# Half-product operands built one step at a time, more pairs by seven half products, and two weight sums made by adding transfers

## The chip, the cores and the metric

The kernel runs on one core of a Trainium2 chip. The metric is the device time of one execution in microseconds (us). A core has a matrix engine (TensorE, PE in the rows; PEld is its weight load), a vector engine (VectorE, DVE), a scalar engine (ScalarE, ACT), a general engine (GpSimd, POOL) and SyncE (SP), which here only starts transfers.

## What is computed

Two decoder layers over 512 positions of width 1024, in float32. Layer 0 mixes with retention and sparse attention, layer 1 with a gated linear recurrence; both end with a SwiGLU feed-forward part, which is all that the change touches:

```python
def swiglu(h, w1, w3, w2):          # D_MODEL 1024, D_FF 2816
    return (jax.nn.silu(h @ w1) * (h @ w3)) @ w2
...
    h = rmsnorm(x, norm_ffn_g[layer])
    x = x + swiglu(h, ffn_w1[layer], ffn_w3[layer], ffn_w2[layer])
```

## The kernel before

**Precision.** Each float32 operand is split into a rounded high part and a low remainder, and a product is three matmuls: high weights by high data (L129), high by low (L130), low by high (L131). `load_split` (L105) loads 512 KB of weights into one of two `raw` buffers (L109, SyncE), casts 128x512 halves to `whi` on ACT (L116) and subtracts to get `wlo` on DVE (L118).

**The feed-forward part.** `ffn` goes over 22 pairs f of 128 columns of w1 and w3, in two halves of 11; each half ends with `residual_out`, 8 blocks of 33 matmuls that multiply by w2. A pair comes in two forms. The *normal* form projects twice (`p_a`, `p_b`): 2 x 8 x 3 = 48 matmuls of 512 columns, with four casts and four subtractions of weights. Then DVE multiplies by the norm factor R (L357), ACT applies silu (L358), DVE makes g (L360), POOL multiplies g by R (L361), and g is split into `gh` and `gl` (L154, L155).

The *seven* form (`seven_products`) treats the two projections as a product of 2x2 block matrices and makes it from seven half products: 7 x 4 x 3 = 84 matmuls of 256 columns, with seven casts and seven subtractions of weights. Four of the seven weight operands are sums, `s1` to `s4`, of the halves a1, a2 (of the pair's `raw_a`) and b1, b2 (of `raw_b`), made on DVE: s1 = b1+b2 (L304), s2 = s1+a1 (L305), s3 = a1+b1 (L314), s4 = s2+a2 (L320). They lie in slab 4 for every other such pair, and in cells 22 to 25 for the rest. The products' results are put together on DVE in 256-column pieces (L313, L319, L325, L329 to L332), then silu (L333), g (L334), and g by R on POOL (L335). `SEVEN` lists the pairs of this form, 11 of 22 in each layer: 2, 4, 6, 8, 10, 11, 13, 15, 17, 19, 21.

On the data side the seven form needs sums of halves of the normalised input, `xu` and `xw`. `seven_operands` makes them once in each layer, for four k: for each k two ACT scalings (L257), four DVE operations of 256 columns (L260 to L263) and two splits (a cast on ACT, a subtraction on DVE, each). It is called ahead of pair 2, for all four k.

**Order.** A scheduler sets the order of each engine's instructions when the kernel is built, from the order of the code and from the buffers; each engine then works through its list strictly in order, and waits where an operand is not there. Transfers started from one engine are started in its order too.

Of the kernel before, what the change touches and what calls it, by code (L numbers as in the profile page):

```python
# [12 lines left out]
FR = mybir.dt.float32r  # L13
BF = mybir.dt.bfloat16
U8 = mybir.dt.uint8
AF = mybir.ActivationFunctionType
ALU = mybir.AluOpType
# [14 lines left out]
def trunk(ctx, tc, t_in, out):  # L32
    nc = tc.nc
# [12 lines left out]
    def slab(i, name, dt=F32):  # L46
        return big.tile([128, 4, 512], dt, name=name, tag=f"B{i}")

    def cell(i, name, dt=F32):
        return big.tile([128, 512], dt, name=name, tag=f"c{i}")  # L50

    def temp(name, dt=F32):
        return tmp.tile([128, 512], dt, name=name, tag="t")
# [16 lines left out]
    xT = [xall[:, k, :] for k in range(KT)]  # L70

    hh = [wp.tile([128, S], FR, name=f"hh{k}", tag=f"hh{k}", bufs=1) for k in range(KT)]
    hl = [wp.tile([128, S], FR, name=f"hl{k}", tag=f"hl{k}", bufs=1) for k in range(KT)]
    gains = main.tile([128, 5, KT], F32, name="gains")
# [78 lines left out]
    def split(dst_h, dst_l, src, eng=None):  # L153
        nc.scalar.copy(dst_h, src)  # L154
        (eng or nc.vector).tensor_tensor(out=dst_l, in0=src, in1=dst_h.bitcast(F32), op=ALU.subtract)  # L155
# [89 lines left out]

    SEVEN = [2, 4, 6, 8, 10, 11, 13, 15, 17, 19, 21]


    def seven_operands(layer, which):
        lo, hi = slice(0, 256), slice(256, 512)
        xs = {1: [], 2: [], 3: [], 4: [], 5: [], 6: [], 7: []}
        for k in range(4):
            x1, x2 = temp(f"x1_{layer}_{k}"), temp(f"x2_{layer}_{k}")
            for x, j in ((x1, k), (x2, k + 4)):
                nc.scalar.activation(out=x, in_=xT[j], func=AF.Copy, scale=gains[:, which, j:j + 1])  # L257
            u, w = temp(f"xu_{layer}_{k}"), temp(f"xw_{layer}_{k}")
            tt = nc.vector.tensor_tensor
            tt(out=u[:, lo], in0=x1[:, lo], in1=x1[:, hi], op=ALU.subtract)  # L260
            tt(out=u[:, hi], in0=x2[:, hi], in1=u[:, lo], op=ALU.add)
            tt(out=w[:, lo], in0=x2[:, lo], in1=u[:, hi], op=ALU.subtract)
            tt(out=w[:, hi], in0=x1[:, hi], in1=x2[:, hi], op=ALU.subtract)  # L263
            U, W = ([cell(6 + 4 * k + 2 * j + i, f"x{n}{layer}_{k}_{i}", FR) for i in range(2)]
                    for j, n in enumerate("uw"))
            split(*U, u)
            split(*W, w)
            for i, part, cs in ((1, (hh[k], hl[k]), lo), (2, (hh[k + 4], hl[k + 4]), lo),
                                (3, (hh[k + 4], hl[k + 4]), hi), (5, U, lo), (6, U, hi), (4, W, lo), (7, W, hi)):
                xs[i].append((part[0][:, cs], part[1][:, cs]))  # L270
        return xs

    def seven_products(layer, f, xs, norm, n):
        w13 = t_in["w13"]
        lo, hi = slice(0, 256), slice(256, 512)
        tt = nc.vector.tensor_tensor
        name = f"{layer}_{f}"
        ra, rb = (wp.tile([128, 1024], F32, name=f"raw_{x}{name}", tag="raw", bufs=2) for x in "ab")
        nc.sync.dma_start(out=ra, in_=w13[layer, 2 * f])
        nc.sync.dma_start(out=rb, in_=w13[layer, 2 * f + 1])  # L280
        a1, a2, b1, b2 = ra[:, 0:512], ra[:, 512:1024], rb[:, 0:512], rb[:, 512:1024]
        if n % 2:
            s1, s2, s3, s4 = (cell(22 + j, f"s{j}_{name}") for j in range(4))
        else:
            q = slab(4, f"s_{name}")
            s1, s2, s3, s4 = (q[:, j, :] for j in range(4))
        ws = {}

        def parts(i, src):
            ws[i] = load_split(None, 512, f"s{i}_{name}", [src])  # L290

        def product(i, o, first):
            ((wh_, wl_),) = ws[i]
            for j, (xh, xl) in enumerate(xs[i]):
                wh, wl = wh_[:, j * 128:(j + 1) * 128], wl_[:, j * 128:(j + 1) * 128]
                mm(o, wh, xh, start=first and j == 0, stop=False, skip_group_check=True)  # L296
                mm(o, wh, xl, start=False, stop=False, skip_group_check=True)  # L297
                mm(o, wl, xh, start=False, stop=j == 3, skip_group_check=True)  # L298

        t1, t2 = cell(26, f"t1_{name}"), cell(27, f"t2_{name}")  # L300
        p1, v, v7 = t1[:, lo], t1[:, hi], t2[:, lo]
        ta, g = temp(f"ta{name}"), temp(f"g{name}")
        parts(1, a1)
        tt(out=s1, in0=b1, in1=b2, op=ALU.add)  # L304
        tt(out=s2, in0=s1, in1=a1, op=ALU.add)  # L305
        o1 = bank("mm", f"p_w{name}")[:, lo]
        product(1, o1, True)
        nc.scalar.copy(p1, o1)
        parts(6, s2)
        o2 = bank("sc", f"p_x{name}")[:, lo]  # L310
        product(6, o2, True)
        parts(2, a2)
        tt(out=v, in0=o2, in1=p1, op=ALU.subtract)  # L313
        tt(out=s3, in0=a1, in1=b1, op=ALU.add)  # L314
        product(2, o1, False)
        parts(7, s3)
        product(7, o2, False)
        parts(5, s1)
        tt(out=v7, in0=o2, in1=p1, op=ALU.subtract)  # L319
        tt(out=s4, in0=s2, in1=a2, op=ALU.add)  # L320
        o3 = bank("sc", f"p_z{name}")[:, lo]
        product(5, o3, True)
        parts(4, b2)
        product(4, o2, False)
        tt(out=g[:, hi], in0=v7, in1=o3, op=ALU.subtract)  # L325
        parts(3, s4)
        product(3, o3, False)
        R = norm.R
        tt(out=ta[:, lo], in0=o1, in1=R[:, lo], op=ALU.mult)  # L329
        tt(out=g[:, lo], in0=o2, in1=p1, op=ALU.subtract)  # L330
        tt(out=ta[:, hi], in0=o3, in1=v, op=ALU.subtract)
        tt(out=ta[:, hi], in0=ta[:, hi], in1=R[:, hi], op=ALU.mult)  # L332
        nc.scalar.activation(out=ta, in_=ta, func=AF.Silu)  # L333
        tt(out=g, in0=g, in1=ta, op=ALU.mult)  # L334
        nc.gpsimd.tensor_tensor(out=g, in0=g, in1=R, op=ALU.mult)  # L335
        return g

    def ffn(layer, norm, norm_next, tail=None):
        w13, w2 = t_in["w13"], t_in["w2"]
        half = NF // 2  # L340
        for f0, f1 in ((0, half), (half, NF)):
            bh = [slab(i, f"gh{layer}_{f0}_{i}", FR) for i in range(2)]
            bl = [slab(2 + i, f"gl{layer}_{f0}_{i}", FR) for i in range(2)]
            gs = [(bh[j // 4][:, j % 4, :], bl[j // 4][:, j % 4, :]) for j in range(8)]
            gs += [(cell(2 * j, f"gh{layer}_{f0}_{j}", FR), cell(2 * j + 1, f"gl{layer}_{f0}_{j}", FR))
                   for j in range(half - 8)]
            for f in range(f0, f1):
                if f == 2:
                    xs = seven_operands(layer, norm.which)
                if f in SEVEN:  # L350
                    g = seven_products(layer, f, xs, norm, SEVEN.index(f))
                else:
                    a = project(w13[layer, 2 * f], f"a{layer}_{f}")
                    R = norm.R if norm.R is not None else norm.factor()
                    b = project(w13[layer, 2 * f + 1], f"b{layer}_{f}", tag="sc")
                    ta = temp(f"ta{layer}_{f}")
                    nc.vector.tensor_tensor(out=ta, in0=a, in1=R, op=ALU.mult)  # L357
                    nc.scalar.activation(out=ta, in_=ta, func=AF.Silu)  # L358
                    g = temp(f"g{layer}_{f}")
                    nc.vector.tensor_tensor(out=g, in0=b, in1=ta, op=ALU.mult)  # L360
                    nc.gpsimd.tensor_tensor(out=g, in0=g, in1=R, op=ALU.mult)  # L361
                split(*gs[f - f0], g)
            end = f1 == NF
            residual_out(w2[layer], f0, f1, gs, norm_next if end else None, f"y{layer}_{f0}_", tail if end else None)
# [53 lines left out]
    for s in range(2):  # L418
        kf = temp(f"kc{s}")
        nc.vector.tensor_tensor(out=kf, in0=first[s], in1=R0, op=ALU.mult)  # L420
        for g in range(2):
            for j2 in range(2):
                nc.sync.dma_start(out=kc2[2 * s + g][j2 * 64:j2 * 64 + 64, 0:S - j2],
                                  in_=kf[g * 64:g * 64 + 64, j2:S])
# [6 lines left out]
    for br in range(2):  # L431
        kf = temp(f"kf{br}")
        nc.vector.tensor_tensor(out=kf, in0=first[2 + br], in1=R0, op=ALU.mult)
        for part, dst in zip(parts(f"kf{br}", kf), (KA, KB)):
            for g in range(2):
                for h in range(2):
                    nc.sync.dma_start(out=dst[h * 64:h * 64 + 64, 2 * br + g, :].bitcast(F32),
                                      in_=part[g * 64:g * 64 + 64].bitcast(F32))
    VVr = VV.rearrange("p (b g) (c h d) -> p b g c h d", b=2, h=2, d=64)
    for br in range(2):  # L440
# [4 lines left out]
        for c in range(4):  # L445
# [4 lines left out]
                                op=ALU.subtract)  # L450
# [7 lines left out]
    for s in range(2):  # L458
        ph = bank("sc", f"h1_{s}")
        for half in range(2):  # L460
            x = cell(12 + 2 * s + half, f"xkv{s}{half}")[:, 0:496].rearrange("p (j g i) -> p j g i", j=8, g=2)
            for g in range(2):
# [3 lines left out]
                    out=x[:, :, g, :], in0=src,  # L466
                    in1=cpos[:, s, 8 * half:8 * half + 8].unsqueeze(2).to_broadcast([128, 8, 31]), op=ALU.add)
# [620 lines left out]
```

## Time and profile before

| | before |
|---|---|
| median of three runs (two of them 1339.71 and 1340.9) | 1340.9 us |
| the profiled execution | 1340.04 us |
| its span, first to last instruction | 1338.3 us |
| PE busy | 1312.1 us, 98% |
| DVE busy | 886.2 us, 66% |
| ACT busy | 581.6 us, 43% |
| POOL busy | 353.6 us, 26% |
| mean granted clock of TensorE | 0.990 of full speed |

Busy shares are means over stages with different limits, so each feed-forward part is read by itself: where its matmuls start, what they wait for, and what DVE and POOL do in the same microseconds. A busy time of matmuls counts their overlap; the time that one takes in a dense row of them is the distance between the starts of two.

### The profile page before, as it was taken

To read this page: it belongs to the slowest core of one execution; us is meant where nothing else is said; L and a number is where in the kernel's file an instruction comes from. 1 tells how busy PE (TensorE), PEld (TensorE's weight loads), DVE (VectorE), ACT (ScalarE), POOL (GpSimd) and SP (SyncE) were. 2 spreads that over 40 slices of the span, in tenths; PEclk is the share of its full clock that TensorE was granted. 3 is DMA by queue.
4 is the path that set the end of the run, shared out by engine and by line. 5 is a ranking of instruction groups with operands and counts; after the bars stand their busy time and mean duration, and the time that the engine had idled before them with its cause. 6 is when DMAs were issued, how large, how long until landed. Compare 5 with 4: busy or idle time off the path is not lost.

```text
span 1338.3 us, 19686 instructions
## 1 busy us (share of the span) xinstructions
PE 1312.1 (98%) x7385; PEld 1132.7 (85%) x7385; DVE 886.2 (66%) x1586; ACT 581.6 (43%) x1095; POOL 353.6 (26%) x373
## 2 busy tenths in 40 slices
PE   9999999999899999999999999999989999999998
PEld 8788888887789888998888888888868988899987
DVE  5636776756777447786469786774776863587742
ACT  5346656554534223443443343332553432344443
POOL 0126675321001000111147655551200110011111
PEclk9999999999899999999999999999989999999999
DMA  7741111032233332324322222221312323333332
GB/s 258 183 133 49 32 48 48 16 111 79 63 95 106 104 93 92 113 94 131 108 83 89 64 63 64 65 78 48 110 52 91 110 86 105 95 111 95 91 108 85
DMA packets 40383, 122.08 MB, mean 91 GB/s; under 512 B 5408, under 2 KB 9952, under 8 KB 40160
## 3 DMA queue, kind: packets, MB, share of 16 engines
q1 hardware_dynamic: 40144, 120.57, 29.4%
q8 instruction: 58, 0.95, 0.3%
q14 instruction: 37, 0.30, 0.1%
q10 hardware_dynamic: 144, 0.26, 0.1%
HBM read 113.47 MB, written 2.10 MB: 86 GB/s over the span
## 4 chain that ended last, share of the span: by engine, by line
PE 78%; DVE 2%; ACT 1%; issue 1%; POOL 1%; POOLq 0%; DVEq 0%; ACTq 0%
PE y L130 6%; PE y L129 6%; PE y L131 6%; PE p_a L129 3%; PE p_a L130 3%; PE p_a L131 3%; PE p_b L129 3%; PE p_b L130 3%; PE p_b L131 3%; PE p_x L296 2%; PE p_x L297 2%; PE p_x L298 2%; PE mo L129 2%; PE mo L130 2%; PE mo L131 2%; PE lv L885 2%
## 5 line engine op out<-in xcount | busy, mean ns | idle before, releaser
L335 POOL TENSOR_TENSOR g<-g,R 128x512 f32<-128x512 f32 x22 | 29.0, 1320 | 516.7 <-DVE g L334 516.7
L131 PE MATMUL y<-gh,wlo_y 128*128 128x512 f32 (+1 forms) x363 | 138.4, 383 | 0.0
L130 PE MATMUL y<-gl,whi_y 128*128 128x512 f32 (+1 forms) x363 | 138.3, 383 | 0.0
L129 PE MATMUL y<-gh,whi_y 128*128 128x512 f32 (+1 forms) x363 | 137.7, 383 | 0.0
L118 DVE TENSOR_TENSOR wlo_y<-raw_y,whi_y 128x512 fp32r<-128x512 f32 (+1 forms) x96 | 62.3, 659 | 87.1 <-ACT whi_y L116 85.0
L116 ACT CAST whi_y<-raw_y 128x512 fp32r<-128x512 f32 (+1 forms) x96 | 55.2, 585 | 133.4 <-PE y L130 58.1
L116 ACT CAST whi_s<-s 128x512 fp32r<-128x512 f32 x88 | 54.4, 618 | 90.7 <-DVE s L305 63.1
L129 PEld LDWEIGHTS y<-gh,whi_y 128*128 128x128 f32 x363 | 68.2, 188 | 13.3
L131 PEld LDWEIGHTS y<-gh,wlo_y 128*128 128x128 f32 x363 | 68.2, 188 | 13.1
L130 PEld LDWEIGHTS y<-gl,whi_y 128*128 128x128 f32 x363 | 68.3, 188 | 13.1
L118 DVE TENSOR_TENSOR wlo_s<-s,whi_s 128x512 fp32r<-128x512 f32 x88 | 71.6, 814 | 3.7 <-ACT whi_s L116 3.6
L129 PE MATMUL p_a<-hh,whi_a 128*128 128x512 f32 x176 | 69.8, 396 | 0.1
L130 PE MATMUL p_a<-hl,whi_a 128*128 128x512 f32 x176 | 69.6, 395 | 0.0
L131 PE MATMUL p_a<-hh,wlo_a 128*128 128x512 f32 x176 | 68.9, 391 | 0.0
L129 PE MATMUL p_b<-hh,whi_b 128*128 128x512 f32 x176 | 68.7, 390 | 0.0
L130 PE MATMUL p_b<-hl,whi_b 128*128 128x512 f32 x176 | 68.6, 390 | 0.0
L131 PE MATMUL p_b<-hh,wlo_b 128*128 128x512 f32 x176 | 68.6, 390 | 0.0
L182 POOL TENSOR_TENSOR acc<-acc,sq 128x512 f32<-128x512 f32 x24 | 33.2, 1384 | 132.4 <-ACT sq L181 132.2
L116 ACT CAST whi_b<-raw_b 128x512 fp32r<-128x512 f32 x44 | 27.4, 622 | 67.3 <-PE p_a L130 35.2
L116 ACT CAST whi_s<-raw_a 128x512 fp32r<-128x512 f32 x44 | 27.2, 618 | 64.0 <-PE p_x L297 50.9
L600 POOL TENSOR_TENSOR P<-P,st 128x128 f32<-128x128 f32 (+3 forms) x64 | 45.7, 737 | 34.7 <-DVE st L598 25.9
L895 POOL TENSOR_TENSOR hk<-hk,hT 128x256 f32<-128x256 f32 x48 | 42.3, 887 | 44.0 <-PE lv L885 40.6
(439 smaller groups left out, 4144.7 us busy)
## 6 DMA issues: line engine op xcount, KB each, us to landing
raw_a<-w SPq DMA_DIRECT2D x44, 512.0 KB, 3.5
raw_b<-w SPq DMA_DIRECT2D x44, 512.0 KB, 3.5
raw_y<-w SPq DMA_DIRECT2D x32, 512.0 KB, 3.6
raw_mo<-w_out SPq DMA_DIRECT2D x16, 512.0 KB, 3.5
raw_r<-w_in SPq DMA_DIRECT2D x12, 512.0 KB, 3.6
raw_y<-w SPq DMA_DIRECT2D x32, 192.0 KB, 2.8
raw_hf<-w_in SPq DMA_DIRECT2D x8, 512.0 KB, 3.6
raw_hq<-w_in SPq DMA_DIRECT2D x8, 512.0 KB, 3.5
```

Source lines behind the costliest of these rows:

```text
L116: nc.scalar.copy(hi[:, :m], part)
L118: lo_eng[c // 512 % len(lo_eng)].tensor_tensor(out=lo[:, :m], in0=part, in1=hi[:, :m].bitcast(F32), op=ALU.subtract)
L129: mm(o, wh, xh, start=first and j == 0, stop=False)
L130: mm(o, wh, xl, start=False, stop=False)
L131: mm(o, wl, xh, start=False, stop=last and j == n - 1)
L182: (eng or nc.gpsimd).tensor_tensor(out=self.acc, in0=self.acc, in1=sq, op=ALU.add)
L296: mm(o, wh, xh, start=first and j == 0, stop=False, skip_group_check=True)
L297: mm(o, wh, xl, start=False, stop=False, skip_group_check=True)
L298: mm(o, wl, xh, start=False, stop=j == 3, skip_group_check=True)
L335: nc.gpsimd.tensor_tensor(out=g, in0=g, in1=R, op=ALU.mult)
L600: nc.gpsimd.tensor_tensor(out=Ps[x][:, 0:n], in0=Ps[x][:, 0:n], in1=st[:, 6 + x:7 + x].to_broadcast([128, n]), op=ALU.mult)
L895: nc.gpsimd.tensor_tensor(out=k4[:, :, 0, :], in0=k4[:, :, 0, :], in1=t2[:, :, 1:2].to_broadcast([128, npair, B]), op=ALU.mult)
```

## The change

1. The operands `xu` and `xw` are made one k at a time, in calls ahead of pairs 1, 2, 3 and 4, in buffers that the sums of weights use later (slab 4 for odd k, cells 22 to 25 for even k).
2. `SEVEN` has 15 of 22 pairs in each layer: 4, 5, then 7 to 12, 14 to 16, and 18 to 21. Pairs of the seven form now follow one another: in the first half 4-5 and 7-10, in the second 11-12, 14-16 and 18-21.
3. The sums s1 and s3 are no longer made on DVE. Each is a plain transfer of 256 KB from DRAM started by SyncE, and a second transfer of 256 KB, started by POOL, that adds to what the first has put there. b1, b2 and a1 are thus read from DRAM a second time for the sums.

```diff
-    SEVEN = [2, 4, 6, 8, 10, 11, 13, 15, 17, 19, 21]
+    SEVEN = [4, 5, 7, 8, 9, 10, 11, 12, 14, 15, 16, 18, 19, 20, 21]
-    def seven_operands(layer, which):
+    def seven_operands(layer, which, k, xs):
-        for k in range(4):
-            x1, x2 = temp(f"x1_{layer}_{k}"), temp(f"x2_{layer}_{k}")
...
+        if k % 2:
+            q = slab(4, f"x_{layer}_{k}")
+            x1, x2, u, w = (q[:, j, :] for j in range(4))
+        else:
+            x1, x2, u, w = (cell(22 + j, f"x{j}_{layer}_{k}") for j in range(4))
...
     def seven_products(layer, f, xs, norm, n):
...
+        nc.sync.dma_start(out=s1, in_=w13[layer, 2 * f + 1, :, 0:512])
+        nc.sync.dma_start(out=s3, in_=w13[layer, 2 * f, :, 0:512])
+        nc.gpsimd.dma_start(out=s1, in_=w13[layer, 2 * f + 1, :, 512:1024], accum_op=ALU.add)
+        nc.gpsimd.dma_start(out=s3, in_=w13[layer, 2 * f + 1, :, 0:512], accum_op=ALU.add)
...
-        tt(out=s1, in0=b1, in1=b2, op=ALU.add)
         tt(out=s2, in0=s1, in1=a1, op=ALU.add)
...
-        tt(out=s3, in0=a1, in1=b1, op=ALU.add)
...
     def ffn(layer, norm, norm_next, tail=None):
...
-                if f == 2:
-                    xs = seven_operands(layer, norm.which)
+                if 0 < f < 5:
+                    seven_operands(layer, norm.which, f - 1, xs)
```

In the changed kernel the lines behind the four transfers stand 3 to 6 further down: the sums s2 and s4 are L310 and L324, the pieces of the result L318, L323, L329 and L333 to L336, g is L338 and g by R L339 (normal pairs: L362, L365, L366); the operands are L260 and L262 to L265, the plain transfers L289 and L290, the adding ones L291 and L292.

**Place 1, DVE, the operands in layer 0.** A row is a line, an operation, and the result and its inputs; the number behind `xu_` or `x_0_` tells k. In the kernel before, these rows stand behind pair 2's first sums, inside that pair:

```order
L260 TENSOR_TENSOR xu_2_3691<-x_0_2_3687 128x256
L155 TENSOR_TENSOR xw_1_1_3682<-xw_1_3674,xw_1_0_3681 128x512
L261 TENSOR_TENSOR xu_2_3691<-x_0_2_3688,xu_2_3691 128x256
L263 TENSOR_TENSOR xw_2_3692<-x_0_2_3687,x_0_2_3688 128x256
L262 TENSOR_TENSOR xw_2_3692<-x_0_2_3688,xu_2_3691 128x256
L155 TENSOR_TENSOR xu_2_1_3698<-xu_2_3691,xu_2_0_3697 128x512
L260 TENSOR_TENSOR xu_3_3709<-x_0_3_3705 128x256
```

In the changed kernel the operands stand among the last blocks of the mixer's output projection (`mo`) and the weights of pairs 0 and 1:

```order
L155 TENSOR_TENSOR xu_1_1_3677<-x_1_3669,xu_1_0_3676 128x512
L238 TENSOR_TENSOR xall<-mo_6_3386,xall 128x512
L118 TENSOR_TENSOR wlo_b_0_0_3535<-raw_b_0_3531,whi_b_0_0_3533 128x512
L171 SCALAR_TENSOR_TENSOR hl_88<-xall,gains,hh_80 128x512
L155 TENSOR_TENSOR xw_1_1_3679<-x_1_3669,xw_1_0_3678 128x512
L262 TENSOR_TENSOR x_0_0_3575<-x_0_0_3573 128x256
L265 TENSOR_TENSOR x_0_0_3576<-x_0_0_3573,x_0_0_3574 128x256
L118 TENSOR_TENSOR wlo_b_0_512_3539<-raw_b_0_3531,whi_b_0_512_3537 128x512
```

All four k are through on DVE ahead of the weights of pair 2, and other work stands between their rows, where before they stood in one piece behind the start of the first seven pair.

**Place 2, DVE, between two seven pairs of one run, layer 0.** `wlo_s_0_8` are the low parts of pair 8's seven weight operands, `s_9` the sums of pair 9. Before, pair 21 after the normal pair 20, with its two sums at the head:

```order
L304 TENSOR_TENSOR s_21_6272<-raw_b_21_6269 128x512
L314 TENSOR_TENSOR s_21_6272<-raw_a_21_6268,raw_b_21_6269 128x512
L118 TENSOR_TENSOR wlo_s_0_21_0_6279<-raw_a_21_6268,whi_s_0_21_0_6277 128x512
L305 TENSOR_TENSOR s_21_6272<-s_21_6272,raw_a_21_6268 128x512
L331 TENSOR_TENSOR ta_19_6056<-p_z_19_6135,t_0_19_6054 128x256
L357 TENSOR_TENSOR ta_20_6260<-p_a_20_6190,R_3528 128x512
```

Now pair 9 after pair 8; the first of these rows is the last read of a half of `raw_a_8`, whose buffer `raw_a_9` takes:

```order
L118 TENSOR_TENSOR wlo_s_0_8_0_4437<-raw_a_8_4383,whi_s_0_8_0_4435 128x512
L118 TENSOR_TENSOR wlo_s_0_8_0_4454<-s_0_8_4389,whi_s_0_8_0_4452 128x512
L118 TENSOR_TENSOR wlo_s_0_8_0_4470<-s_0_8_4387,whi_s_0_8_0_4468 128x512
L334 TENSOR_TENSOR g_7_4252<-p_x_7_4276,t_0_7_4249 128x256
L118 TENSOR_TENSOR wlo_s_0_8_0_4489<-raw_b_8_4384,whi_s_0_8_0_4487 128x512
L310 TENSOR_TENSOR s_9_4533<-s_9_4533,raw_a_9_4529 128x512
L335 TENSOR_TENSOR ta_7_4251<-p_z_7_4328,t_0_7_4249 128x256
L118 TENSOR_TENSOR wlo_s_0_8_0_4506<-s_0_8_4390,whi_s_0_8_0_4504 128x512
L324 TENSOR_TENSOR s_9_4533<-s_9_4533,raw_a_9_4529 128x512
L336 TENSOR_TENSOR ta_7_4251<-ta_7_4251,R_3528 128x256
L318 TENSOR_TENSOR t_0_8_4395<-p_x_8_4422,t_0_8_4395 128x256
L118 TENSOR_TENSOR wlo_s_0_9_0_4544<-raw_a_9_4529,whi_s_0_9_0_4542 128x512
```

The two additions at the head are gone, and the rows of three pairs (7, 8, 9) are interleaved; L310 waits for `raw_a_9` and for the adding transfer into `s_9`. From L310 to the last read of a half of `raw_a_9` there are 13 rows, 7 of 512 and 6 of 256 columns.

**Place 3, POOL and SP, the transfers of the sums.** On POOL before, the pairs' products g by R stand alone:

```order
L335 TENSOR_TENSOR g_6_4172<-g_6_4172,R_3528 128x512
L361 TENSOR_TENSOR g_7_4378<-g_7_4378,R_3528 128x512
L335 TENSOR_TENSOR g_8_4394<-g_8_4394,R_3528 128x512
L361 TENSOR_TENSOR g_9_4600<-g_9_4600,R_3528 128x512
L335 TENSOR_TENSOR g_10_4613<-g_10_4613,R_3528 128x512
```

Now, at the same pairs, an adding transfer is a row named DMA:

```order
L366 TENSOR_TENSOR g_6_4235<-g_6_4235,R_3528 128x512
L291 DMA s_9_4533<-w 128x512
L292 DMA s_9_4533<-w 128x512
L292 DMA s_0_10_4678<-w 128x512
L291 DMA s_0_10_4676<-w 128x512
L339 TENSOR_TENSOR g_7_4252<-g_7_4252,R_3528 128x512
L291 DMA s_11_5240<-w 128x512
```

Four adding transfers stand ahead of pair 7's product on POOL, and each waits for the plain transfer into the same place. On SP, where those are started:

```order
L289 DMA s_9_4533<-w 128x512
L290 DMA s_9_4533<-w 128x512
L280 DMA raw_a_9_4529<-w 128x1024
L290 DMA s_0_10_4678<-w 128x512
L289 DMA s_0_10_4676<-w 128x512
L281 DMA raw_b_9_4530<-w 128x1024
```

Two plain transfers have come to each seven pair in SP's list, between the loads of `raw_a` and `raw_b`; those into slab 4 (`s_9`) wait until the last operand of pair 7 has been split.

## Rows read from the trace of the kernel before

**Rows 1.** Page, first part: busy time, share of span, instructions by engine.
```profile
PE 1312.1 (98%) x7385; PEld 1132.7 (85%) x7385; DVE 886.2 (66%) x1586; ACT 581.6 (43%) x1095; POOL 353.6 (26%) x373
```
**Rows 2.** Waits of PE: instruction, what it waited for, us in total, times, longest.
```profile
PE p_x L296 <- ACT xu L154: 9.0, 6, 2.7
```
**Rows 3.** Timeline of PE: start, duration, instruction; where feed-forward halves begin, and small matmuls.
```profile
303.54 0.39 PE L129 MATMUL p_a<-hh,whi_a 128*128 128x512 f32 x1
311.02 0.95 PE L202 MATMUL ss<-ones,acc 128*128 128x1 f32 x8
317.63 1.05 PE L216 MATMUL rb<-ident,r 128*128 128x128 f32 x8
493.20 0.28 PE L296 MATMUL p_w<-hh,whi_s 128*128 128x256 f32 x1
668.16 0.39 PE L129 MATMUL p_hf<-hh,whi_hf 128*128 128x512 f32 x1
960.57 0.39 PE L129 MATMUL p_a<-hh,whi_a 128*128 128x512 f32 x1
1151.04 0.28 PE L296 MATMUL p_w<-hh,whi_s 128*128 128x256 f32 x1
```
**Rows 4.** Windows: length, busy PE, PEld, DVE, ACT, POOL; clock, DMA share, GB/s.
```profile
330.00:335.00 5.00, 2.56 (x18) 2.16 (x18) 4.81 (x11) 3.53 (x6) 0.00 (x0) 1.00 0.36 108
335.00:340.00 5.00, 3.01 (x10) 2.28 (x11) 4.76 (x12) 4.33 (x8) 0.00 (x0) 0.62 0.01 2
480.00:600.00 120.00, 120.00 (x735) 108.12 (x735) 87.82 (x145) 48.05 (x85) 13.17 (x9) 1.00 0.32 100
```
**Rows 5.** Timeline of PE: a normal pair's second projection, then a seven pair.
```profile
571.75 0.39 PE L129 MATMUL p_b<-hh,whi_b 128*128 128x512 f32 x1
577.20 0.28 PE L296 MATMUL p_w<-hh,whi_s 128*128 128x256 f32 x1
584.40 0.40 PE L129 MATMUL p_a<-hh,whi_a 128*128 128x512 f32 x1
```
**Rows 6.** Groups by line, layer 0's feed-forward part: operands, one sum (count, busy, mean ns).
```profile
L257 ACT ACTIVATE x<-xall,gains 128x512 f32<-128x512 f32 x8 | 5.6, 718 | 0.7 <-DVE xw L262 0.7
L155 DVE TENSOR_TENSOR xu<-xu,xu 128x512 fp32r<-128x512 f32 x4 | 2.8, 690 | 0.0
L261 DVE TENSOR_TENSOR xu<-x,xu 128x256 f32<-128x256 f32 x4 | 1.7, 426 | 0.1
L304 DVE TENSOR_TENSOR s<-raw_b 128x512 f32<-128x512 f32 x11 | 7.6, 692 | 7.3 <-DMA raw_b<-w 7.3
```
**Rows 7.** Timeline of DVE in a seven pair: start, duration, instruction, idle time before it.
```profile
508.70 0.68 DVE L314 TENSOR_TENSOR s<-raw_a,raw_b 128x512 f32<-128x512 f32 x1
509.30 0.68 DVE L118 TENSOR_TENSOR wlo_s<-raw_a,whi_s 128x512 fp32r<-128x512 f32 x1
512.04 0.41 DVE L332 TENSOR_TENSOR ta<-ta,R 128x256 f32<-128x256 f32 x1
512.37 0.68 DVE L118 TENSOR_TENSOR wlo_s<-s,whi_s 128x512 fp32r<-128x512 f32 x1
515.38 1.40 DVE L118 TENSOR_TENSOR wlo_s<-s,whi_s 128x512 fp32r<-128x512 f32 x1
516.71 1.78 DVE L118 TENSOR_TENSOR wlo_s<-raw_b,whi_s 128x512 fp32r<-128x512 f32 x1
```
**Rows 8.** Timeline of POOL in the same stretch.
```profile
514.94 1.30 POOL L335 TENSOR_TENSOR g<-g,R 128x512 f32<-128x512 f32 x1 [72.34 <-DVE g L334]
516.19 1.76 POOL L361 TENSOR_TENSOR g<-g,R 128x512 f32<-128x512 f32 x1
```
**Rows 9.** DMA issues: transfer, engine, count, KB each, median us from issue to landing.
```profile
raw_a<-w SPq DMA_DIRECT2D x44, 512.0 KB, 3.5
raw_y<-w SPq DMA_DIRECT2D x32, 192.0 KB, 2.8
cw<-cmp_w SPq DMA_DIRECT2D x4, 256.0 KB, 6.7
```

More of the change, by code (lines that the diff above doesn't have):

```diff
@@ L244, in residual_out @@
                     tail(cs)
-    SEVEN = [2, 4, 6, 8, 10, 11, 13, 15, 17, 19, 21]
-    def seven_operands(layer, which):
+    SEVEN = [4, 5, 7, 8, 9, 10, 11, 12, 14, 15, 16, 18, 19, 20, 21]
+    def seven_operands(layer, which, k, xs):
         lo, hi = slice(0, 256), slice(256, 512)
-        xs = {1: [], 2: [], 3: [], 4: [], 5: [], 6: [], 7: []}
-        for k in range(4):
-            x1, x2 = temp(f"x1_{layer}_{k}"), temp(f"x2_{layer}_{k}")
[L256 to L271, printed above, removed]
@@ new lines, in seven_operands @@
+        if k % 2:
[3 more added lines that the diff above has]
+            x1, x2, u, w = (cell(22 + j, f"x{j}_{layer}_{k}") for j in range(4))
+        for x, j in ((x1, k), (x2, k + 4)):
+            nc.scalar.activation(out=x, in_=xT[j], func=AF.Copy, scale=gains[:, which, j:j + 1])
+        tt = nc.vector.tensor_tensor
+        tt(out=u[:, lo], in0=x1[:, lo], in1=x1[:, hi], op=ALU.subtract)
+        tt(out=u[:, hi], in0=x2[:, hi], in1=u[:, lo], op=ALU.add)
@@ new lines, in seven_operands @@
+        tt(out=w[:, lo], in0=x2[:, lo], in1=u[:, hi], op=ALU.subtract)
+        tt(out=w[:, hi], in0=x1[:, hi], in1=x2[:, hi], op=ALU.subtract)
+        U, W = ([cell(6 + 4 * k + 2 * j + i, f"x{n}{layer}_{k}_{i}", FR) for i in range(2)]
+                for j, n in enumerate("uw"))
+        split(*U, u)
+        split(*W, w)
+        for i, part, cs in ((1, (hh[k], hl[k]), lo), (2, (hh[k + 4], hl[k + 4]), lo),
+                            (3, (hh[k + 4], hl[k + 4]), hi), (5, U, lo), (6, U, hi), (4, W, lo), (7, W, hi)):
+            xs.setdefault(i, []).append((part[0][:, cs], part[1][:, cs]))
@@ L340, in ffn @@
         half = NF // 2
+        xs = {}
         for f0, f1 in ((0, half), (half, NF)):
```

## The prediction

> **What bounds the kernel now.** I read the page's busy shares first: PE is busy 98% of the span, the next engine, DVE, 66% [rows 1]. So PE sets the time, and a change gains only where PE does less or stops waiting. Next, PE's waits: in the feed-forward parts the largest is for the casts of `xu`, 9.0 us in six waits of up to 2.7 us [rows 2]. The windows show where and why: at 330 to 340 us PE is busy about half the time and DVE nearly all of it, and from 335 us the granted clock falls to 0.62 [rows 4]. That is the burst of operands inside the first seven pair. For comparison, the 120 us of the second half have 120.00 us of busy PE at clock 1.00 [rows 4]: nothing to gain there but work.
>
> What the burst costs comes from the starts of the halves [rows 3]. Layer 0's first half lasts 493.20 - 303.54 = 189.66 us, its second 668.16 - 493.20 = 174.96. The first has one normal pair more and one seven pair fewer (0.82 us, below) and two groups of small matmuls (0.95 + 1.05 = 2.0) [rows 3]; by work it should last 177.78. So 11.9 us are lost. Layer 1's first half, 1151.04 - 960.57 = 190.47, loses 12.7. Together **24.6 us**: waits for the operands, and matmuls at the lower clock behind them.
>
> **The change, part by part.**
>
> *Seven form in place of normal, four more pairs per layer.* 24 matmuls of 512 columns take 577.20 - 571.75 = 5.45 us, so 48 take 10.90; the 60 matmuls of 256 columns of the seven pair behind them (the other 24 come later, between the next pair's) take 584.40 - 577.20 = 7.20, or 0.120 each, so 84 take 10.08 [rows 5]. A pair saves 0.82 us, eight pairs **6.6 us**.
>
> *Operands in four steps.* For one k, DVE has four half operations of 0.42 and two splits of 0.69, 3.1 us as durations, and ACT two scalings of 0.72 and two casts, about 2.7 [rows 6]; four k are 12 and 11 us. In one piece they stand between PE and its weights. Now they stand among the last output blocks of the mixer and the first two pairs. A normal pair there costs DVE seven 512-column operations: four weight subtractions, L357, L360, one `gl`. Such operations start 0.60 apart, 256-column ones 0.33 [rows 7], so that is 4.2, about 5.0 with its share of the overlap below, against 10.9 of PE. The operand steps of one k (2.5 us by these distances) fit beside each pair. I count the whole 24.6 us as saved; if the cover is gone in layer 1, whose first pairs share DVE with the norm, I allow 0 to 2 us back.
>
> *The sums on DVE.* In a seven pair DVE has four sums, seven subtractions, g and `gl`, 13 x 0.60 = 7.8, and seven pieces, 7 x 0.33 = 2.3. Two subtractions take 1.40 and 1.78 instead of 0.68 [rows 7], just while POOL multiplies two g by R [rows 8]: 1.8 us more for two pairs, 0.9 for one. Together 11.0 us, more than PE's 10.08. Alternating with normal pairs this was covered; in a run it would not be. Without s1 and s3 it is **9.8 us, 97% of PE's time**: covered, barely.
>
> *The runs.* Alternation gave DVE and the transfers a pause after each seven pair; a run does not. The tightest loop that I find goes through `raw_a`: its buffer is free at the last read of pair n's half, the next load lands 3.5 us later [rows 9], L310 waits for it, and from there to the last read of the new half DVE has 7 x 0.60 + 6 x 0.33 = 6.2 us (order, place 2), with the overlap 7.1. That is 9.7 to 10.6 per pair against 10.08: a loss of 0 to 0.5 at a step inside a run; with loads queued behind the new plain transfers 0.9 (0.4 more, from SP's list at place 3, an estimate). There are 10 such steps per layer (1 + 3 in the first half, 1 + 2 + 3 in the second), 20 in all: 0 to 18 us. Each run starts with some slack and about half the steps pay 0.5 or a little over: I take **6 us**.
>
> *Adding transfers.* No row of before shows one. The nearest rows: 192 KB land in 2.8 us, 256 KB from `cmp_w` in 6.7 [rows 9]. In most pairs the place is free a whole pair ahead. Tight are the pairs that take slab 4 two pairs after another inside a half: 7 to 9, 14 to 16, 19 to 21, six places in all. From the split that frees the slab to L310, DVE alone has seven 512-column and four 256-column rows in its order, 5.5 us; PE has five groups of 12 matmuls, 5 x 12 x 0.120 = 7.2, between the product with that last operand and the one that needs s2. With DVE a little ahead of PE I count 8. The plain transfer takes some 3 of these, so an adding transfer, with its start on POOL, has about 5: at 2.8 plus a start of about 1.3 (taken from POOL's product [rows 8]) it is in time; at 6.7 it is 3 late, 18 us over six places. I take the lower price, since size and target are nearer to the 192 KB loads, and keep the upper for the range. The Trainium skill, DMA: Bandwidth & Descriptors, section Anatomy of one DMA, gives 2.0 us plus bytes over 436 GB/s for transfers started from GpSimd, an estimate of 2.6 us for 256 KB; no run here shows it, and the sum would stay.
>
> *POOL's list.* Four adding transfers stand ahead of pair 7's product there (place 3). POOL is busy 13.17 of 120 us [rows 4], so room is not the question, but their waits hold the product back, and ACT's cast to `gh` stands ahead of casts of weights. Inside about 1.5 us this is covered; it is part of the 0 to 18 above.
>
> *Sum.* 1340.0 (profiled execution; the median of the runs is 0.9 higher) - 24.6 - 6.6 = 1308.8; + 6 in the runs = **1315 us**.
>
> **The rivals.**
>
> A, the forecast: the burst's stall goes, runs pay a little. 1310 to 1321, chance 0.48.
>
> B, runs pay nothing: DVE's 9.8 and the loop's 9.7 stay under 10.08. 1309. For it: PE was never late in the second half before, which has a seven pair in every two. Against: there DVE had 16 us of work in 21, now nearly 10 in 10. Chance 0.23.
>
> C, the adding transfers come late, at 6.7 us or held up in their start: 1308.8 + 18, with a few us of the runs less where one wait covers the other, 1322 to 1330; a wait of 2.7 us was followed by the lower clock [rows 2, 4], which would add. What could hold them up is seen for a product on POOL: with DVE reading two operands, the two engines' operations lengthen together (1.40 and 1.78 for 0.68) [rows 7, 8]. If starting a transfer suffers alike, it adds 1 us or so at each of six places, 6 us. The Trainium skill, SBUF — State Buffer, section SBUF: two separate sides, warns of this ("DVE blocks DMA"), and in Who interferes with whom lets an addition of two SBUF operands block only what POOL reads, not the writing of descriptors. By the first the sum would be about 1321, by the second 1315; the rows show the block for products only. Chance of C 0.17.
>
> E, the operands' stall comes back elsewhere: DVE at 4.8 of 5 us [rows 4] is the kind of stretch that the steps now bring to the end of the mixer. If half of the 24.6 returns, 1327 to 1332. Against: the operands need no weights and nothing waits for them before pair 4. Chance 0.06.
>
> D, the other side: an adding transfer holds POOL until it lands. Then POOL has 2t + 1.3 per seven pair [rows 8]. Up to t = 4.4 this is under 10.08 and costs nothing; above, each of the 20 steps inside a run pays the difference. To be slower by 2% (1367) 58 us are needed, 2.9 a step, t = 5.8; at 6.7 [rows 9] it is 4.6 a step, 1309 + 92 = 1401. For it: the place needs the plain transfer first and POOL's list is strict. Against: SP's loads start without waiting for the ones before. Chance 0.06.
>
> **How the numbers follow.** The likeliest is A: 1315. A, B and C without its upper end reach from 1306 (B with 3 us of error in the losses) to 1330, and hold about 0.85; D and the tail of E are left out. The likeliest alone spans 1310 to 1321. A measurement of this kernel can tell about 2% from no change; 2% faster is 1314.1, just under the forecast. B is faster, of A a little under half, of C and E nothing: faster 0.45. Same is the rest of A, C, E: 0.49. Slower is D: 0.06.
>
> **What would show each step right or wrong.** In the profile of the changed kernel: PE's waits for `xu` casts gone, and the windows around both layers' first pairs with PE busy throughout and clock 1.00. Starts of the halves: the first 24.6 us shorter over both layers, apart from the pairs' saving. In the runs, DVE near 98% busy and small waits of PE for ACT casts or `wlo` of seven pairs; L310 on DVE waiting for `raw_a` (A) or for `s` (C). Adding transfers of 3 us (A, B) or near 6 (C, D). POOL waiting for its own transfers, with PE waiting for g, is D. My prediction is wrong if PE still waits for operands ahead of pair 4, or if a seven pair in a run takes clearly more than 10.7 us.

## The result and the profile after

The changed kernel takes 1351.7 us (median of four runs, 1349.9 to 1353.6) against 1340.4 before (median of four, of which one took 2635 us; the ratio goes by the other three, 1339.7 to 1340.9); the ratio is 1.0086, with a 95% interval of 1.0068 to 1.0104. It is slower by about 0.9%, where 1315 was forecast, in a range of 1306 to 1330. The page of the profiled execution (1353.6 us), busy time, share of the span and instructions by engine, answers to [rows 1]:

```profile
span 1351.7 us, 20618 instructions
PE 1310.4 (97%) x7673; PEld 1146.3 (85%) x7673; DVE 905.1 (67%) x1630; ACT 602.2 (45%) x1127; POOL 404.4 (30%) x433
```

PE's waits (instruction, what it waited for, us in total, times, longest) answer to [rows 2]:

```profile
PE p_w L302 <- ACT t L313: 18.8, 6, 5.3
PE rb L216 <- POOL r L209: 3.3, 1, 3.3
PE p_x L302 <- DVE t L318: 2.3, 4, 0.8
```

and the waits of DVE's sum s2 (L310) behind them:

```profile
DVE s L310 <- DMA raw_a<-w: 30.2, 22, 2.8
DVE s L310 <- DMA s<-w: 17.6, 4, 5.5
```

The waits for the casts of `xu` are gone. In their place PE waits 18.8 us, in six places, for `t`, the copy of a seven pair's first product, and once for the norm. Four of the six, 17.1 us, come where L310 waits for an adding transfer into slab 4: at pairs 9 and 16 of both layers. The other two, 1.0 and 0.7 us, come at pair 20, where L310 waits for `raw_a`. At pair 21, which the forecast counted among the tight places, L310 does not wait for `s`. The transfers (KB each, median us from issue to landing), beside [rows 9]:

```profile
raw_a<-w SPq DMA_DIRECT2D x44, 512.0 KB, 3.5
s<-w SPq DMA_DIRECT2D x60, 256.0 KB, 4.1
s<-w POOLq DMA_DIRECT2D x60, 256.0 KB, 6.0
```

An adding transfer takes 6.0 us to landing in the median, a plain one of the same size 4.1.

Windows (length, busy PE, PEld, DVE, ACT, POOL; granted clock, DMA share, GB/s): the start of layer 0's feed-forward part, the first bad place, and layer 1's start. Beside [rows 4]:

```profile
303.00:380.00 77.00, 77.00 (x428) 67.45 (x427) 53.38 (x92) 37.00 (x63) 17.05 (x15) 1.00 0.55 150
390.00:395.00 5.00, 4.87 (x41) 4.67 (x39) 2.34 (x4) 1.86 (x3) 1.78 (x2) 1.00 0.69 170
395.00:400.00 5.00, 0.00 (x0) 0.00 (x0) 1.28 (x3) 0.22 (x1) 0.86 (x1) 0.72 0.95 232
400.00:405.00 5.00, 4.79 (x26) 4.79 (x27) 3.94 (x7) 1.92 (x4) 2.13 (x2) 0.60 0.71 129
980.00:985.00 5.00, 1.70 (x8) 1.24 (x7) 1.29 (x2) 0.70 (x2) 2.82 (x3) 0.93 0.92 276
```

Where the burst of operands stood, PE is now busy 77.00 of 77 us. But from 395 to 400 it does nothing at all, and in the 5 us behind that the mean granted clock is 0.60. The timelines of that place (start, duration, instruction, idle time before it and what ended it), first SyncE and POOL:

```profile
386.43 0.33 SPq L289 DMA_DIRECT2D s<-w  x1
...
390.94 0.88 POOL L291 DMA_DIRECT2D s<-w  x1 [6.62 <-DVE wlo_s L118]
```

then DVE, ACT and PE:

```profile
385.73 0.68 DVE L118 TENSOR_TENSOR wlo_s<-s,whi_s 128x512 fp32r<-128x512 f32 x1
398.72 0.69 DVE L310 TENSOR_TENSOR s<-s,raw_a 128x512 f32<-128x512 f32 x1 [5.46 <-DMA s<-w]
399.33 0.42 DVE L335 TENSOR_TENSOR ta<-p_z,t 128x256 f32<-128x256 f32 x1
399.78 0.37 ACT L313 COPY t<-p_w 128x256 f32<-128x256 f32 x1 [5.81 <-DVE ta L335]
400.21 0.58 PE L302 MATMUL p_w<-hh,whi_s 128*128 128x256 f32 x1 [5.34 <-ACT t L313]
```

The times to landing of the plain transfer of 386.43 and of the adding one of 390.94:

```profile
s<-w SPq DMA_DIRECT2D x1, 256.0 KB, 3.9
s<-w POOLq DMA_DIRECT2D x1, 256.0 KB, 7.8
```

This is the step from pair 8 to pair 9, in slab 4 that pair 7 has just left. The last split of pair 7 ends at 386.4, and SyncE starts the plain transfer at once. It lands 3.9 us later, at 390.4, and POOL starts the adding one 0.56 us behind that, at 390.9, as it does behind most plain transfers in this trace (the row above names a weight split that ended between the two). The landing of the adding transfer releases L310 at 398.7, 7.8 us after its start. L310 is pair 9's sum and is not needed by PE for three more groups of twelve matmuls. But behind it in DVE's list stands L335, which is the last reader of pair 7's `t`; pair 8's copy of `p_w` goes to the same place and waits for it; and PE cannot go on adding to that `p_w` before it is copied. So a late operand of the next pair stops the product that is running.

### The profile page after: what moved, and what is told of

The parts are those of the page before. It is cut to its first block, busy times and chain, and to the rows that moved or that the text cites. A ratio compares the mean times of both kernels' runs of the same rounds, so it can differ in the third digit from the quotient of the medians.

```text
span 1351.7 us, 20618 instructions
## 1 busy us (share of the span) xinstructions
PE 1310.4 (97%) x7673; PEld 1146.3 (85%) x7673; DVE 905.1 (67%) x1630; ACT 602.2 (45%) x1127; POOL 404.4 (30%) x433
## 3 DMA queue, kind: packets, MB, share of 16 engines
q0 software_dynamic: 8640, 15.73, 7.1%
## 4 chain that ended last, share of the span: by engine, by line
PE 68%; DVE 6%; DMA 5%; issue 2%; POOL 1%; ACT 1%; DVEq 0%; POOLq 0%; ACTq 0%
PE y L129 6%; PE y L130 6%; PE y L131 6%; DMA s<-w 3%; PE p_x L302 3%; PE p_x L303 2%; PE p_x L304 2%; DMA raw_a<-w 2%; PE p_w L302 2%; PE lv L890 2%; PE p_w L304 2%; PE p_w L303 2%; PE mo L129 2%; PE mo L130 2%; PE mo L131 2%
## 5 line engine op out<-in xcount | busy, mean ns | idle before, releaser
L116 ACT CAST whi_s<-s 128x512 fp32r<-128x512 f32 x120 | 74.4, 620 | 79.4 <-PE p_z L303 21.2
L118 DVE TENSOR_TENSOR wlo_s<-s,whi_s 128x512 fp32r<-128x512 f32 x120 | 91.9, 766 | 23.3 <-ACT whi_s L116 22.8
L291 POOL DMA_DIRECT2D s<-w x30 | 26.9, 897 | 251.7 <-DVE ta L333 145.4
L302 PE MATMUL p_w<-hh,whi_s 128*128 128x256 f32 x240 | 71.8, 299 | 19.7 <-ACT t L313 18.8
L339 POOL TENSOR_TENSOR g<-g,R 128x512 f32<-128x512 f32 x30 | 44.8, 1494 | 145.7 <-DVE g L338 145.7
L302 PE MATMUL p_x<-xw,whi_s 128*128 128x256 f32 x240 | 70.4, 293 | 2.3 <-DVE t L318 2.3
L304 PE MATMUL p_w<-hh,wlo_s 128*128 128x256 f32 x240 | 70.9, 295 | 0.0
L303 PE MATMUL p_w<-hl,whi_s 128*128 128x256 f32 x240 | 70.6, 294 | 0.0
L304 PE MATMUL p_x<-xw,wlo_s 128*128 128x256 f32 x240 | 69.5, 290 | 0.0
L303 PE MATMUL p_x<-xw,whi_s 128*128 128x256 f32 x240 | 69.5, 290 | 0.0
L302 PEld LDWEIGHTS p_w<-hh,whi_s 128*128 128x128 f32 x240 | 48.8, 203 | 21.7 <-ACT t L313 20.2
```

Source lines behind the costliest of these rows:

```text
L116: nc.scalar.copy(hi[:, :m], part)
L118: lo_eng[c // 512 % len(lo_eng)].tensor_tensor(out=lo[:, :m], in0=part, in1=hi[:, :m].bitcast(F32), op=ALU.subtract)
```

## The experiments

Times are medians with the ratio to the kernel before (about 1340) and its 95% interval; line numbers of a kernel differ by a few from those of the changed one. The first four take the change apart.

**Operand steps alone.** All 15 pairs and all transfers undone:

```diff
-    SEVEN = [4, 5, 7, 8, 9, 10, 11, 12, 14, 15, 16, 18, 19, 20, 21]
+    SEVEN = [4, 6, 8, 10, 11, 13, 15, 17, 19, 21]
-        nc.sync.dma_start(out=s1, ...)      # and the three others
+        tt(out=s1, in0=b1, in1=b2, op=ALU.add)
...
+        tt(out=s3, in0=a1, in1=b1, op=ALU.add)
```

> The kernel before with the operands in four steps alone: sums on DVE, no adding transfers, pairs of the seven form alternating (4, 6, 8, 10, then 11, 13, ... 21: ten per layer, one fewer than before, since they start at pair 4). Theory (the tight adding transfers cost the time, the operand steps gain what was forecast): 1340 - 24.6 + 1.6 = 1317 us, no PE wait for xu. Rival (the operands' stall comes back at the start of the feed-forward parts whatever is done with the sums; in the changed kernel layer 1 lost about 6 us there): 1323 us or more, with the loss at 960 to 1000 us. Rival (the steps gain nothing): 1340.

Measured: 1322.2 us, 0.9866 (0.9851 to 0.9881). No wait for `xu`, 1.0 us at most lost at either layer's start, and one stall that the forecast had not, of 4.5 us by the distances of matmul starts, at 588 to 600 us. PE's wait there:

```profile
PE p_z L299 <- DVE wlo_s L118: 2.0, 1, 2.0
```

and the rows of DVE there:

```profile
591.39 1.37 DVE L118 TENSOR_TENSOR wlo_s<-s,whi_s 128x512 fp32r<-128x512 f32 x1
592.68 1.77 DVE L118 TENSOR_TENSOR wlo_s<-raw_b,whi_s 128x512 fp32r<-128x512 f32 x1
```

There two splits fall on two products of POOL, as in [rows 7, 8]. There the same cost PE nothing, so why PE is late here is not shown; with the sums taken off DVE and the same pairs (below) the stall is gone. Less 4.5 us the kernel would stand at 1317.7, close to the theory's 1317. The rival falls: the operands' stall does not come back.

**Sums on DVE again, pairs and steps as changed** (the four transfers out, the two additions in).

> The changed kernel with s1 and s3 made on DVE again; runs of seven pairs and operand steps as in the changed kernel. Theory (late adding transfers): the stalls of 4 to 9 us at 7-9, 14-16 and 19-21 go; what is left is DVE at 11.0 us against 10.08 in a run, about 0.9 at each of 20 steps, 18 us: 1309 + 18 = 1327 us, every seven pair in a run near 11 us. Rival (the runs themselves cost the time, by raw loads and DVE, the adding transfers are not to blame): the same 1350 or more, with stalls at the same places.

Measured: 1336.0 us, 0.997 (0.9959 to 0.9981). It is neither the theory's 1327 nor the rival's 1350. The long stalls are gone; PE waits up to 1.4 us at each of twelve places for DVE:

```profile
PE p_x L297 <- DVE t L320: 11.7, 12, 1.4
```

Runs do need the sums off DVE: 1336.0 - 1308.8 = 27 us, if all of it is put on the 20 steps, is 1.4 each, more than the 0.9 expected. But the transfers as placed cost 16 us more than the additions they replace.

**Plain in place of adding.**

```diff
-        nc.gpsimd.dma_start(out=s1, in_=w13[layer, 2 * f + 1, :, 512:1024], accum_op=ALU.add)
+        nc.gpsimd.dma_start(out=s1, in_=w13[layer, 2 * f + 1, :, 512:1024])
```

> The changed kernel with POOL's second transfers made plain: they overwrite instead of adding, so the sums s1 and s3 are left out (what lands is b2 or b1 alone). Theory A (the adding is what takes 6.0 us instead of 4.1): landing of POOL's transfers falls to about 4, each tight place stalls some 2 to 3 us less, 1351 - 15 = about 1336 us. Theory B (the start from POOL and the sharing of queues with other loads take it): landing stays near 6 and the time near 1351.

Measured: 1336.6 us, 0.9976 (0.9964 to 0.9989). Landing falls from 6.0 to 4.0 us, and the share of the DMA engines' time that POOL's queue takes falls with it. Queue, packets, MB, share; the changed kernel first:

```profile
q0 software_dynamic: 8640, 15.73, 7.1%
```

```profile
q0 software_dynamic: 4800, 15.73, 3.8%
s<-w POOLq DMA_DIRECT2D x60, 256.0 KB, 4.0
```

Theory A holds: adding itself costs 15.1 us of this kernel's time. L310 still waits about 3 us for `s` at the same four places.

**Without the second transfers.** L291 and L292 are left out.

> The changed kernel without POOL's second transfers: s1 and s3 are what the plain transfers bring (b1 and a1), so the two sums are left out; everything else, runs and operand steps, as in the changed kernel. Theory (the second transfer's start, its wait for the first and the adding are the whole loss): the chain is a plain transfer of about 4 us with 8 to spare, no stall over 2 us, DVE at 9.8 of 10.08: 1309 plus 0 to 8, 1313 us. Rival (runs cost time of their own, by raw loads, the queue of SP and DVE at 97%): 1325 us or more, with losses inside the runs.

Measured: 1315.7 us, 0.9818 (0.9802 to 0.9835), no stall over 1 us. So the runs, the steps and the saving of the pairs together give what the forecast said as a sum; the second transfers carry the whole miss, 1351.7 - 1315.7 = 36 us: 20.9 for being there, 15.1 for adding.

The others ask how they cost it.

**Seven pairs in twos.** `SEVEN` is 4, 5, 7, 8, 10, 11, 13, 14, 16, 17, 19, 20.

> The changed kernel with 12 seven pairs per layer in twos (4-5, 7-8, 10-11, 13-14, 16-17, 19-20), so that a place for sums is never used again before three pairs have passed; adding transfers as in the changed kernel. Theory (only the reuse after two pairs is too short for plain plus adding transfer, about 4 + 7 us): no stall over 2 us in the runs, 1340 - 24.6 - 1.6 + 6 (layer 1's start, as in the changed kernel) = 1320 us. Rival (adding transfers disturb everywhere): 1335 or more.

Measured: 1331.2 us, 0.9929 (0.9912 to 0.9946). Not the 1320 expected. One stall of 2.7 us is left and small ones of 0.7 to 1.4 us at six places; layer 1's start loses 5.0. L310 waits for `s` nowhere in this profile, but up to 2.7 us for `raw_a` at 21 of 24 pairs. The early reuse is not the only cause.

**Alternating pairs with adding transfers**: as with operand steps alone, but the sums by transfers.

> The changed kernel with alternating pairs (4, 6, 8, 10, 11, 13, ... 21); sums by adding transfers, operands in four steps. Beside the kernel with operand steps alone (1322.2 us, same pairs) it differs in the sums only. Theory (adding transfers cost only where the place is reused early, and through POOL's list ahead of the norm's r at layer 1's start, about 5 us): 1322 to 1327 us. Rival (they also take work off DVE that matters): 1317. Rival (they disturb the other loads everywhere): 1332 or more.

Measured: 1322.6 us, 0.9868 (0.9854 to 0.9883). In both feed-forward parts only layer 1's start loses time: 5.0 us at 960 to 980, and 1.0 ahead of that as with the steps alone. The stall at 588 to 600 is gone. Where a place is free early, adding transfers cost PE nothing.

**The norm's power ahead of them in POOL's list**, pairs as in the last one.

```diff
+        with tc.issue_after(norm.power) if f < 9 else ExitStack():
             nc.gpsimd.dma_start(out=s1, in_=w13[layer, 2 * f + 1, :, 512:1024], accum_op=ALU.add)
```

> Alternating pairs with operand steps and adding transfers (1322.6 us), with the first adding transfers of each layer kept behind the norm's power (L209) in POOL's list. Theory (PE's wait of 3.1 us for r at layer 1's start, with the lower clock behind it, comes from POOL standing at an adding transfer that waits for its place): the loss of 5 us at 960 to 980 us goes, 1317.6 us. Rival (r is late for another reason, the operand steps on DVE and ACT at the end of the mixer): 1322.

Measured: 1318.2 us, 0.9836 (0.982 to 0.9853), and no loss at 960 to 980. Shown. It is also 4.0 us less than the operand steps alone with the same pairs, so at these pairs the sums by transfers are worth something once POOL's list is in order. What the order removes is in POOL's timeline of the changed kernel:

```profile
974.58 0.87 POOL L292 DMA_DIRECT2D s<-w  x1 [2.21 <-DVE wlo_a L118]
982.16 0.86 POOL L291 DMA_DIRECT2D s<-w  x1 [6.70 <-DMA s<-w]
982.72 1.35 POOL L209 TENSOR_TENSOR r<-ms,mhalf 128x4 f32<-128x4 f32 x1
```

The input of r was there at 977.3 (DVE's L206 starts at 977.11 and takes 0.15); POOL stood until 982.2 before an adding transfer into slab 4, whose plain transfer was still under way.

**Two places for t1 and t2.**

```diff
-        t1, t2 = cell(26, f"t1_{name}"), cell(27, f"t2_{name}")
+        t1, t2 = (cell(26 + j + 2 * (n % 2), f"t{j + 1}_{name}") for j in range(2))
```

> The changed kernel with two places instead of one for t1 and t2, so that the copy of p_w does not wait for L335, which stands behind L310 on DVE. Theory (the late adding transfer itself is needed by the product with s2, some 12 to 22 matmuls later): PE's waits move from p_w to p_x and shrink by 1.4 to 2.6 us at six places, about 1351 - 10 = 1341 us. Rival (the single place of t turns a harmless delay of L310 into a stall): 1320 us or less.

Measured: 1349.0 us, 1.0069 (1.0054 to 1.0084), 2.7 us less than the changed kernel, whose interval overlaps this one. Neither the theory's 1341 nor the rival's 1320 holds, and PE's new waits say why:

```profile
PE p_w L304 <- DVE wlo_s L118: 10.2, 4, 3.5
PE p_z L304 <- DVE wlo_s L118: 9.5, 4, 3.1
```

With `t` out of the way, PE waits for weight splits that stand behind L310 as well. The single place of `t` is only the first thing that L310 holds up.

**L310 behind the pair before.** Only DVE's order is changed:

```diff
+        with ExitStack() as later:
+            for ins in behind:          # L318 and the last weight split of the seven pair before
+                later.enter_context(tc.issue_after(ins))
             tt(out=s2, in0=s1, in1=a1, op=ALU.add)
```

> The changed kernel with one more constraint on DVE's order: the sum s2 of a seven pair (L310) stands behind the last weight split and the first piece (L318) of the seven pair before it, so that its wait for a late adding transfer does not hold those up. Theory (the lateness is one thing, what stands behind L310 on DVE another, and both are paid): a part of the stalls of 4 to 5 us at six places goes, since PE has two to three groups of 1.44 us more to do; 6 x 3 us and the lower clock behind them, 1351 - 20 = 1331 us. Rival (PE needs s2 just as early, as with two places for t, which gained 2.7 us): 1346 us or more.

Measured: 1327.6 us, 0.991 (0.9891 to 0.9928), 24 us less, with not a byte or a buffer changed. At the same place of pair 9 L335's counterpart now runs before the sum, and the sum waits 0.65 us (3.1 at the worst place, pair 9 of layer 1):

```profile
393.04 0.42 DVE L343 TENSOR_TENSOR ta<-p_z,t 128x256 f32<-128x256 f32 x1 [0.21 <-PE p_z L307]
395.51 0.69 DVE L316 TENSOR_TENSOR s<-s,raw_a 128x512 f32<-128x512 f32 x1 [0.65 <-DMA s<-w]
```

**Three sets of places.** s4 is made in the place of s2, and every third seven pair takes cells 25, 28 and 29:

```diff
-        if n % 2:
-            s1, s2, s3, s4 = (cell(22 + j, f"s{j}_{name}") for j in range(4))
+        if n % 3:
+            s1, s3, s2 = (cell(c, f"s{c}_{name}") for c in ((22, 23, 24) if n % 3 == 1 else (25, 28, 29)))
...
+        s4 = s2
```

> The changed kernel with three sets of places for the sums instead of two (s4 is made in the place of s2, so a set is three places), and nothing else; a place is used again after three pairs or more. Theory (the adding transfers cost only where the place is used again after two pairs): the stalls at 7-9, 14-16 and 19-21 go, what stays is layer 1's start and the runs' own loss, 1315.7 + 5 = 1321 us. Rival (four transfers a pair, the adding ones with 6 us to landing, are late or disturb raw loads whatever the place): 1335 or more.

Measured: 1335.8 us, 0.9965 (0.9949 to 0.998), ten runs from 1330 to 1341. This is the rival's number, though L310 no longer waits for `s`; PE still waits 9.6 us for `t` and 4.4 for the norm. **With the norm's power ahead as well:**

> As the kernel with three sets of places, and the first adding transfers of each layer kept behind the norm's power in POOL's list. Theory: 1316 us, both kinds of stall gone, which is what the kernel without the second transfers takes (1315.7). Rival: no better than three sets alone.

Measured: 1328.3 us, 0.9915 (0.99 to 0.9929), not 1316. L310 waits no longer for `s`, but it does for `raw_a`, and holds the same things up:

```profile
PE p_w L304 <- ACT t L315: 12.5, 9, 2.5
DVE s L312 <- DMA raw_a<-w: 30.9, 27, 2.5
```

**All three**: places, power and DVE's order.

> Three sets of places, the norm's power ahead in POOL's list, and the sum s2 (L310) behind the pair before on DVE: all three causes found so far taken away, pairs and adding transfers as in the changed kernel. Theory (the 12 us that three sets with the power ahead still lose are waits of L310 for raw_a, which hold up L335 and so the copy of p_w): PE's waits of p_w for t go, 1316 to 1319 us. Rival (adding transfers slow the loads of raw_a so far that pairs in a run cannot follow one another in 10.1 us): 1325 us or more, with PE waiting for p_x instead.

Measured: 1316.1 us, 0.9823 (0.9808 to 0.9838). PE's waits for `t` are gone; L310 waits for `raw_a` 10.4 us in 12 times, at no cost that the time shows. **Order and power, two sets of places:**

> The changed kernel (two sets of places, late adding transfers at six places) with the norm's power ahead in POOL's list and the sum s2 behind the pair before on DVE. Theory (causes add up): 1327.6 - 5 = 1322.6 us; what it loses to the kernel with three sets besides is what the lateness alone costs once nothing else stands behind it, some 4 to 7 us. Rival (the place is the larger cause): 1327 or more.

Measured: 1324.1 us, 0.9877 (0.9858 to 0.9897). So two sets of places, with the lateness that is left, cost 1324.1 - 1316.1 = 8 us more than three, where the four runs of this kernel lie between 1320.8 and 1326.3.

**Operand steps ahead of pairs 0 and 1, the pairs of before, sums on DVE.**

> The kernel before with its own 11 pairs and sums on DVE, and the operands made in four steps, two ahead of pair 0 and two ahead of pair 1. Theory (the steps fit around the mixer's end, and nothing else costs): 1322.2 (operand steps, ten pairs) - 1.6 = 1320.6 us. Rival (pair 2 as first seven pair comes too early for DVE, which still has the norm's work): a stall of some us at the start of each feed-forward part, 1325 to 1335.

Measured: 1317.4 us, 0.9832 (0.9818 to 0.9847); 2.4 us are lost at 940 to 980 us. This kernel and the one with all three repairs are 1.7 to 1.8% faster than before and cannot be told apart. So the operand steps alone have the whole gain that these runs show; four more pairs and the transfers, even with all three repairs, add none that can be measured.

## Why the prediction was wrong

**Right: what bounded the kernel, and the operands' 24.6 us.** Steps alone gave 17.8 us with one pair fewer per layer (1.6) and a new stall of 4.5: 23.9 in all. With the pairs of before they gave 23. E, that half of the stall comes back elsewhere, did not happen. The price of the burst, read from the starts of the halves, holds within 2 us.

**Right as a sum: 6.6 us gained by the pairs, 6 lost in the runs.** Without second transfers the kernel takes 1315.7, and with them and all three repairs 1316.1; the sum less all losses was 1308.8, so 6.9 and 7.3 were lost, near A's 6 and not B's nothing. No run shows the two terms apart.

**Wrong: the step "Adding transfers".** It took the lower price, 2.8 us and a start of 1.3, "since size and target are nearer to the 192 KB loads". Landing is 6.0 us, 7.8 at the place shown, and the plain transfer ahead of it took 4.5 until POOL started the next, where 3 were taken. The upper bound of 6.7 that was kept for the range is near the truth: at four of the six places L310 waits 3.6 to 5.5 us, 17.6 in all, for the 18 of the upper price. But even that is half of the 36 that the transfers cost. The Trainium skill, DMA: Bandwidth & Descriptors, section Anatomy of one DMA, gives an estimate of 2.6 us for 256 KB; the plain transfer from POOL took 4.0 and the adding one 6.0 here, and the measurement decides.

**Wrong, and the larger error: lateness was counted at the operand, not at what stands behind it.** The budget of 8 us ran to the product that needs s2. The forecast's own order fence of place 2 shows L335, a weight split and L318 behind L310, and the rows of the loop were counted for their time, never asked who waits for them. L335 frees `t`, `t` the copy of `p_w`, and that stops a product three groups of matmuls earlier. Taken by itself, the order gave 24 us. For shares that add up, the power alone in the changed kernel is estimated, as no run has it: 1351.7 - 4.4 (its gain at alternating pairs) = 1347.3. From there the order is worth 1347.3 - 1324.1 = 23 us, two thirds of the miss, and a third set of places behind it 8. Three sets without the order give 1347.3 - 1328.3 = 19, since then only the shorter waits for `raw_a` stand before the same rows; the two overlap by 11 us.

**Wrong: POOL's list "inside about 1.5 us".** The forecast looked at g there and not at the norm's r, ahead of which layer 1 has adding transfers that wait for a place. It cost 4.4 us at alternating pairs, and 3.5 and 7.5 in the other two kernels where the power was moved ahead.

**The clock adds to it.** PE's waits in both feed-forward parts are 28 us (18.8 for `t`, 3.3 for r, six groups of 0.3 to 2.3), but the kernel lies 1351.7 - 1308.8 = 43 us above the sum without losses. After 5.3 us without a matmul the mean granted clock was 0.72 and then 0.60 (windows above), and matmuls of 256 columns followed at 0.21 instead of 0.12. In the six stretches at the lower of the two clock levels (1.2 instead of 2.4 GHz) in these parts the starts of matmuls lie 11 us further apart in sum than in dense rows at the higher. The forecast named this for rival C and added nothing for it.

**The rivals.** C was right in kind, at 1322 to 1330, and far too small; its second half, that the start of a transfer suffers from DVE, is wrong. In the changed kernel the 24 starts on POOL during which DVE was busy at least 90% of the time took 0.88 us in the median, the 13 with DVE busy less than half 0.87. On the other side, 58 DVE additions and subtractions of 512 columns that overlap such a start and no product take 684 ns in the median, 694 at most, against 685 and 712 for those that overlap nothing; beside a product on POOL they go up to 1823, and up to 2610 beside a product and a start. The Trainium skill, SBUF — State Buffer, section Who interferes with whom, says that such an addition blocks what POOL reads and not the writing of descriptors; the trace agrees with both halves. The trap that the forecast quotes from that page's section SBUF: two separate sides is told by the Trainium skill of DVE operations in a 2-port mode, which such an addition does not have, so by neither section would the sum have moved from 1315. D did not happen: POOL is free again 0.9 to 1.2 us after it begins to start a transfer.

## What to carry to other kernels

When a change makes an operand arrive later, find the instruction that waits for it, list what stands behind it on its engine, and take the earliest deadline among those, not the operand's own. An instruction that may wait belongs behind everything that the running work needs; moving one such sum gave 24 us here. A transfer of a new kind is priced at the upper bound until a run has shown it, with the chain that it adds (place free, plain transfer, adding transfer) laid against the time until the place is used again.

## What the runs showed of the hardware

An adding transfer takes 1.9 times the DMA engines' time of a plain one of the same bytes (7.1% against 3.8% for 15.73 MB) and 1.8 times the packets (8640 against 4800). In the changed kernel POOL starts most adding transfers 0.56 us after the plain one into the same place has landed. Plain transfers of 256 KB of weights, mostly started in twos, land after 4.1 us, those of 512 KB after 3.5. At 395 to 400 us the DMA engines were 95% busy with 232 GB/s. In the kernel before 100 GB/s took a share of 0.32 [rows 4]; by that, an estimate from bytes alone would have been 0.74, and would have shown room that was not there.
